# Eight of sixteen feature tiles of the retention output by seven products, and sums of stored tiles by GpSimd's queue

## The chip, the cores and the metric

One core of one Trainium2 chip runs the whole kernel in one launch. The metric is the time of one execution on the device in microseconds (us). The engines of the core are TensorE (PE, with its weight loads as PEld), VectorE (DVE), ScalarE (ACT), GpSimd (POOL) and SyncE (SP). Each runs its own instructions in order, and SP, ACT and POOL can issue DMA transfers from their own queues.

## The reference

Two layers over a sequence of 1024 tokens with 1024 features, batch 1, in float32: layer 0 mixes by forgetting attention, layer 1 by retention, and each is followed by a SwiGLU network with 2816 hidden features. The change lies mostly in retention:

```python
def retention(h, w_in, w_out):          # 4 heads, 512 value features each
    ...                                 # q, k, v, g from h @ w_in; q, k rotated
    _, y = lax.scan(step, state0, (qc, kc, vc))       # chunks of 64 tokens
    y = y.transpose(1, 0, 3, 2, 4).reshape(B, S, H, dv)
    mu = jnp.mean(y, axis=-1, keepdims=True)
    var = jnp.mean(jnp.square(y - mu), axis=-1, keepdims=True)
    y = ((y - mu) * lax.rsqrt(var + EPS)).reshape(B, S, H * dv).astype(h.dtype)
    return (jax.nn.silu(g) * y) @ w_out               # 2048 -> 1024 features

def swiglu(h, w_in, w_out):
    gu = h @ w_in
    return (jax.nn.silu(gu[..., :D_FF]) * gu[..., D_FF:]) @ w_out

def reference(x, ...):
    for i in range(DEPTH):
        h = rmsnorm(x, norm_mix[i])
        x = x + (forgetting_attention if i % 2 == 0 else retention)(h, ...)
        x = x + swiglu(rmsnorm(x, norm_ffn[i]), ffn_w_in[i], ffn_w_out[i])
    return rmsnorm(x, final_norm)
```

## The kernel before, in words

Activations lie with features on the 128 partitions and tokens along the free axis, in tiles of 128x512 (a half of the tokens, h = 0 or 1). Every float32 operand of TensorE is split in two parts, hi and lo: ACT casts the hi part (L98) and DVE subtracts it from the source to leave lo (L99). A product of two operands is then three matmuls, hi by hi, hi by lo and lo by hi. The plain form is `mm_u` (L101, matmuls at L106 to L108).

Most of the large projections don't use the plain form. They take a 2x2 block of (feature tiles x token halves) at a time and compute it by seven products instead of eight: `Blocks` loads four weight blocks A11 to A22 into two 128x1024 staging tiles (tag `st`, five buffers) and forms the sums S1 to S4 on DVE; the activations' side has B11, T1, T2, B21, T3, T4, B22, where the T's are sums of tiles of one feature pair; and `Products` (matmuls at L645 to L647) runs the seven pairs, each over four tiles of the inner dimension and three matmuls, into three PSUM banks. `Stored` keeps the seven activation operands of one group in DRAM; its `get` lands them in place by `landed`: a DMA on SP's queue writes the float32 tile into the buffer that will be lo, ACT casts hi out of it and DVE subtracts in place.

Each SwiGLU network stores its first 16 hidden tiles as two such groups (`stored[0]`, `stored[1]`, DRAM tiles named ac), and `paired_out` multiplies them with the output weights. Group 0 is landed while the last products of the input projection still run, group 1 while the last product of group 0 runs. The other six hidden tiles (ad) go through `mm_u`.

The retention layer runs eight stages (4 heads x 2 token halves). In `finish` of a stage ACT copies four value tiles out of PSUM, squares are summed, TensorE sums over the partitions (L159) and later spreads the per-token factors over all partitions (L165, tile rw in PSUM), DVE multiplies the four tiles by them (L1153) and they are stored to DRAM as zd. The gate silu(g) lies in DRAM as gd. For head 0 DVE multiplies it in at once (L1157); for the other 12 tiles it is loaded beside zd afterwards and DVE multiplies 128x1024 at a time (L801). The output projection is two passes over eight of the sixteen feature tiles each: the first (the loop at the end of the listing) is plain, eight output tiles x two halves x eight input tiles x three matmuls, and adds the residual xo; the second is `out_proj`, also plain.

The order of the instructions on each engine comes from a scheduler that moves them within dependences; the pools (`yp` with 16 buffers, `st` with 5, `bpa` with 32 and `bpb` with 24) limit how far ahead a load can be.

Of the kernel before, what the change touches and what calls it, by code (L numbers as in the profile page):

```python
# [17 lines left out]
P = 128  # L18
# [19 lines left out]
def trunk(ctx, tc, nc, d, out):  # L38
# [62 lines left out]
    def mm_u(ps, wts, acts, h, cols=slice(0, H), first=True, last=True):  # L101
        n = len(wts)
        for k in range(n):
            wh, wl = wts[k]
            xh, xl = (t[:, cols] for t in acts[k][h])
            nc.tensor.matmul(ps, wh, xh, start=(first and k == 0), stop=False)  # L106
            nc.tensor.matmul(ps, wh, xl, start=False, stop=False)  # L107
            nc.tensor.matmul(ps, wl, xh, start=False, stop=(last and k == n - 1))  # L108
# [76 lines left out]
    with ExitStack() as fs:  # L185
# [13 lines left out]
        wk0, wk1 = wtile(d["fox_qk"][1], 4), []  # L199
        for kt in range(KT):  # L200
# [7 lines left out]
            for at, w, idx, k in (0, wk0, 1, 4), (1, wk1, 3, 0), (3, wk1, 3, 4):  # L208
                if kt == at:
                    w += wtile(d["fox_qk"][idx][:, k * P:], 4)  # L210
# [285 lines left out]
    def landed(pool, src):  # L496

        hi, lo = units(pool)
        nc.sync.dma_start(lo.bitcast(F32), src)
# [9 lines left out]
    class Combos:  # L509
# [32 lines left out]
        def get(self, n):  # L542
# [4 lines left out]
    FROM_COMBOS = {"S2": ("B11", "T1", "T2"), "S3": ("B21", "T3"), "S4": ("T4", "B22")}  # L547
    FROM_STORED = {"A11": ("B11",), "S1": ("T1",), "S2": ("T2",), "A12": ("B21",), "S3": ("T3",), "A22": ("T4",),
                   "S4": ("B22",)}

    class Stored:


        def __init__(self, name, pools):
            self.pools = pools
            self.d = {n: dp.tile([P, 4 * H], F32, tag=name + n, name=name + n) for n in NAMES}
# [20 lines left out]

    class Blocks:


        def __init__(self, src):
            self.s1, self.ready = None, {}
            sts = []
            for i in range(2):
                st = sp.tile([P, 1024], F32, tag="st", name=nm("st"), bufs=5)
                nc.sync.dma_start(st, src[:, i * 1024:(i + 1) * 1024])
# [4 lines left out]
        def sums(self, early=False):  # L591
# [6 lines left out]
            nc.vector.tensor_tensor(self.s2, self.s1, self.a11, op=ALU.subtract)  # L598
# [6 lines left out]
        def get(self, n):  # L605
# [8 lines left out]
            if n == "S3":  # L614
                nc.vector.tensor_tensor(self.a21, self.a11, self.a21, op=ALU.subtract)
                return wsplit(self.a21)
            if n == "A12":
                return wsplit(self.a12)
# [51 lines left out]
    def in_turn(srcs, X, use, coming=None):  # L670
# [618 lines left out]
```

## Time and profile before

| | |
|---|---|
| time of the kernel, median of 3 runs | 2588.68 us (2587.34 to 2588.96) |
| time of the profiled execution | 2588.64 us |
| its span in the trace | 2586.9 us |
| TensorE busy | 2560.8 us, 99% of the span |
| DVE, ACT, POOL busy | 1839.0, 1228.3, 170.6 us |
| DMA traffic | 312.13 MB, mean 121 GB/s |

Busy time of TensorE counts overlapping matmuls: one 128x512 matmul lasts 0.39 us in the trace, but they start closer to each other than that, since they are pipelined. So the count of matmuls in a stretch tells its pace better than the busy share. The time of the profiled execution is 1.7 us above the span.

### The profile page before, as it was taken

How to read it: one execution, taken by the hardware profiler on the slowest of the kernel's cores; microseconds unless marked ns; L12 is line 12 of the kernel's file. 1: busy time of each engine (PE TensorE's matmuls, PEld its weight loads, DVE VectorE, ACT ScalarE, POOL GpSimd, SP SyncE). 2: the span in 40 equal slices, each digit the busy share in tenths (PEclk: the TensorE clock that was granted, in tenths of full speed). 3: DMA queues.
4: the chain of work that ended last, by engine and by line, in shares of the span. 5: the costliest groups of instructions: out<-in, count | busy, mean ns of one | idle time of the engine just before them, and what ended most of it. 6: DMA issues, size and time to landing. Idle time of an engine off the chain costs nothing.

```text
span 2586.9 us, 35264 instructions
## 1 busy us (share of the span) xinstructions
PE 2560.8 (99%) x12808; PEld 2182.2 (84%) x12808; DVE 1839.0 (71%) x3131; ACT 1228.3 (47%) x2320; POOL 170.6 (7%) x147
## 2 busy tenths in 40 slices
PE   9999999999999999999999999999999999999998
PEld 8889887888888878889898989898888888888888
DVE  6798888966666678886656576785567666668784
ACT  6566656543333454554343435662354333335543
POOL 0143323000000000001000010000000000000000
PEclk9999999999999999999999999999999999999999
DMA  3111142432332345533332325555522333325541
GB/s 130 45 58 58 58 147 93 152 106 94 114 106 94 122 155 176 166 116 115 102 118 98 110 98 167 184 191 193 202 98 82 110 98 107 103 90 186 175 143 66
DMA packets 145759, 312.13 MB, mean 121 GB/s; under 512 B 16560, under 2 KB 29616, under 8 KB 145584
## 3 DMA queue, kind: packets, MB, share of 16 engines
q1 hardware_dynamic: 144864, 309.33, 35.9%
q8 instruction: 100, 1.64, 0.3%
q14 instruction: 75, 0.61, 0.1%
q10 hardware_dynamic: 720, 0.55, 0.1%
HBM read 217.54 MB, written 92.27 MB: 120 GB/s over the span
## 4 chain that ended last, share of the span: by engine, by line
PE 93%; DVE 2%; DMA 2%; issue 2%; ACT 1%; POOL 0%; SPq 0%; DVEq 0%; POOLq 0%; ACTq 0%
PE mm L645 18%; PE mm L647 18%; PE mm L646 18%; PE mm L106 7%; PE mm L107 7%; PE mm L108 7%; PE mm L765 2%; PE mm L763 2%; PE mm L764 2%; PE mm L256 1%; PE mm L257 1%; PE mm L258 1%; DMA b<-ac_T 1%; PE mm L1116 1%; PE mm L1117 1%
## 5 line engine op out<-in xcount | busy, mean ns | idle before, releaser
L645 PE MATMUL mm<-b,wh 128*128 128x512 f32 x2128 | 826.7, 390 | 2.7 <-ACT b L98 2.7
L646 PE MATMUL mm<-b,wh 128*128 128x512 f32 x2128 | 827.9, 389 | 0.0
L647 PE MATMUL mm<-b,wl 128*128 128x512 f32 x2128 | 825.2, 389 | 0.0
L98 ACT CAST wh<-st 128x512 fp32r<-128x512 f32 (+1 forms) x449 | 276.6, 617 | 499.2 <-PE mm L646 298.3
L645 PEld LDWEIGHTS mm<-b,wh 128*128 128x128 f32 x2128 | 399.4, 188 | 86.5 <-ACT b L98 4.0
L647 PEld LDWEIGHTS mm<-b,wl 128*128 128x128 f32 x2128 | 399.5, 188 | 83.2 <-DVE wl L99 0.4
L646 PEld LDWEIGHTS mm<-b,wh 128*128 128x128 f32 x2128 | 399.6, 188 | 82.1
L99 DVE TENSOR_TENSOR wl<-st,wh 128x512 fp32r<-128x512 f32 (+1 forms) x449 | 318.6, 713 | 180.3 <-ACT wh L98 177.9
L98 ACT CAST wh<-s 128x512 fp32r<-128x512 f32 x252 | 156.5, 622 | 298.5 <-PE mm L646 270.6
L106 PE MATMUL mm<-b,wh 128*128 128x512 f32 x736 | 286.8, 393 | 7.8 <-ACT b L126 5.5
L107 PE MATMUL mm<-b,wh 128*128 128x512 f32 x736 | 287.4, 391 | 1.7 <-DVE b L99 1.7
L108 PE MATMUL mm<-b,wl 128*128 128x512 f32 x736 | 287.4, 391 | 0.0
L99 DVE TENSOR_TENSOR wl<-s,wh 128x512 fp32r<-128x512 f32 x252 | 180.2, 717 | 89.6 <-ACT wh L98 85.5
L106 PEld LDWEIGHTS mm<-b,wh 128*128 128x128 f32 x736 | 138.9, 189 | 37.3 <-ACT b L126 6.2
L107 PEld LDWEIGHTS mm<-b,wh 128*128 128x128 f32 x736 | 138.9, 189 | 29.5 <-DVE b L99 2.2
L108 PEld LDWEIGHTS mm<-b,wl 128*128 128x128 f32 x736 | 138.8, 189 | 28.4
L764 PE MATMUL mm<-wl,b 128*128 128x256 f32 x448 | 126.6, 283 | 0.0
L763 PE MATMUL mm<-wh,b 128*128 128x256 f32 x448 | 126.2, 283 | 0.0
L765 PE MATMUL mm<-wh,b 128*128 128x256 f32 x448 | 126.2, 283 | 0.0
L597 DVE TENSOR_TENSOR s<-st 128x512 f32<-128x512 f32 x84 | 58.2, 692 | 67.8 <-DMA st<-ffn_in 28.8
L98 ACT CAST b<-b 128x512 fp32r<-128x512 f32 x112 | 67.7, 620 | 71.9 <-DMA b<-ac_B 39.2
L99 DVE TENSOR_TENSOR b<-b,b 128x512 fp32r<-128x512 f32 x112 | 75.5, 688 | 33.0 <-ACT b L98 32.6
(500 smaller groups left out, 4019.7 us busy)
## 6 DMA issues: line engine op xcount, KB each, us to landing
st<-ffn_in SPq DMA_DIRECT2D x88, 512.0 KB, 3.5
st<-ffn_out_pairs SPq DMA_DIRECT2D x32, 512.0 KB, 3.6
b<-ac_T SPq DMA_DIRECT2D x64, 256.0 KB, 5.8
ac_T<-t SPq DMA_DIRECT2D x48, 256.0 KB, 2.4
b<-ac_B SPq DMA_DIRECT2D x48, 256.0 KB, 5.0
st<-fox_qk SPq DMA_DIRECT2D x32, 256.0 KB, 2.7
xo<-xd SPq DMA_DIRECT2D x32, 256.0 KB, 3.0
ac_B<-t SPq DMA_DIRECT2D x32, 256.0 KB, 2.4
```

What stands on the lines that cost most here:

```text
L98: nc.scalar.copy(hi, src)
L99: return nc.vector.tensor_tensor(lo, src, hi.bitcast(F32), op=ALU.subtract)
L106: nc.tensor.matmul(ps, wh, xh, start=(first and k == 0), stop=False)
L107: nc.tensor.matmul(ps, wh, xl, start=False, stop=False)
L108: nc.tensor.matmul(ps, wl, xh, start=False, stop=(last and k == n - 1))
L597: nc.vector.tensor_tensor(self.s1, self.a21, self.a22, op=ALU.add)
L645: nc.tensor.matmul(ps, hi[:, js], th, start=first and j == 0, stop=False, skip_group_check=True)
L646: nc.tensor.matmul(ps, hi[:, js], tl, start=False, stop=False, skip_group_check=True)
L647: nc.tensor.matmul(ps, lo[:, js], th, start=False, stop=(j == 3), skip_group_check=True)
L763: nc.tensor.matmul(o, th[:, tk], hi[:, js], start=f, stop=False, skip_group_check=True)
L764: nc.tensor.matmul(o, th[:, tk], lo[:, js], start=False, stop=False, skip_group_check=True)
L765: nc.tensor.matmul(o, tl[:, tk], hi[:, js], start=False, stop=(j == 3), skip_group_check=True)
```

## The change

Five parts.

1. The first pass of the retention output projection (now over heads 0 and 1) is done by seven products: `Blocks(w, True)` takes four weight tiles by strided loads, `Products` runs over them with a `Stored` group zc, and y is formed from the residual xo by adding or subtracting the products. Signs are chosen so that `finish` stores some tiles negated. The second pass (heads 2 and 3) stays plain.
2. The operands T1 to T4 of zc aren't computed on DVE: after each of heads 0 and 1, `zc.add` makes each by two transfers of GpSimd's queue, a copy from DRAM to DRAM and a transfer that adds to what lies there (16 transfers of 128x1024). SP loads the operands during and after the last three stages.
3. All 32 gate multiplies are moved into `finish` and onto GpSimd; the 8 at L1157 and the 12 at L801 on DVE go.
4. In each SwiGLU network, group 0 is loaded through staging tiles (128x1024 on SP) and then split; group 1 is still landed in place, but by GpSimd's queue (28 transfers of 128x512 in each network). So are eight tiles zd of the second pass, 128x512 each.
5. At the start the first weight load on SP is 128x128 instead of 128x512. At the end ACT copies the last tile's residual into PSUM before its matmuls, which then add to it; ACT squares straight from PSUM, and the column sum takes that square by matmuls of its own, two to a block of tokens where there was one.

```diff
-    def colsum(acc, mp, mtag, nb=4):
+    def colsum(acc, mp, mtag, nb=4, more=None):
...
-            nc.tensor.matmul(ps[:, b:b + 1], acc[:, b * P:(b + 1) * P], ones[:, 0:1], start=True, stop=True)
+            nc.tensor.matmul(ps[:, b:b + 1], acc[:, b * P:(b + 1) * P], ones[:, 0:1], start=True, stop=more is None)
+            if more is not None:
+                nc.tensor.matmul(ps[:, b:b + 1], more[:, b * P:(b + 1) * P], ones[:, 0:1], start=False, stop=True)
...
-        wk0, wk1 = wtile(d["fox_qk"][1], 4), []
+        wk0, wk1 = wtile(d["fox_qk"][1], 1), []
...
-    def landed(pool, src):
+    def landed(pool, src, queue):
...
-        nc.sync.dma_start(lo.bitcast(F32), src)
+        queue.dma_start(lo.bitcast(F32), src)
...
     class Stored:
...
+        def add(self, js, n, a, b):
+
+            c = slice(js.start * H, js.stop * H)
+            nc.gpsimd.dma_start(self.d[n][:, c], self.d[a][:, c])
+            nc.gpsimd.dma_start(self.d[n][:, c], self.d[b][:, c], accum_op=ALU.add)
+
         def get(self, n):
             if n not in self.t:
-                self.t[n] = [landed(self.pools[n], self.d[n][:, j * H:(j + 1) * H]) for j in range(4)]
+                if not self.staged:
+                    self.t[n] = [landed(self.pools[n], self.d[n][:, j * H:(j + 1) * H], self.queue) for j in range(4)]
+                    return self.t[n]
+                self.t[n] = []
+                for i in range(2):
+                    st = sp.tile([P, 1024], F32, tag="st", name=nm("st"), bufs=5)
+                    nc.sync.dma_start(st, self.d[n][:, i * 1024:(i + 1) * 1024])
+                    self.t[n] += [bsplit(self.pools[n], st[:, HALF[j]]) for j in range(2)]
             return self.t[n]
...
-        stored = [Stored(f"ac{i}_{g}_", pools) for g in range(2)]
+        stored = [Stored(f"ac{i}_{g}_", pools, g == 0) for g in range(2)]
...
+                if c1 == S and n == KT - 1:
+                    nc.scalar.copy(ps, u)
+                    mm_u(ps, ws[n], acts, h, cs, first=False, free=True)
+                    sq = sp.tile([P, H], F32, tag="sc", name=nm("sq"), bufs=4)[:, :wid]
+                    nc.scalar.activation(sq, ps, AF.Square)
+                    cps = colsum(norm.acc[h][:, cs], mp, "ms", nb, sq)
...
         for vt in range(4):
-            nc.vector.tensor_tensor(ys[vt], ys[vt], fb, op=ALU.mult)
-            if h < 1:
-                g = yu("g")
-                nc.sync.dma_start(g, gd[4 * h + vt][:, HALF[ib]])
-                nc.vector.tensor_tensor(ys[vt], ys[vt], g, op=ALU.mult)
-            nc.sync.dma_start(zd[4 * h + vt][:, HALF[ib]], ys[vt])
+            g = yu("g")
+            nc.sync.dma_start(g, gd[4 * h + vt][:, HALF[ib]])
+            if h < 2 and vt % 2 != ib:
+                nc.vector.scalar_tensor_tensor(ys[vt], ys[vt], -1.0, fb, op0=ALU.mult, op1=ALU.mult)
+            else:
+                nc.vector.tensor_tensor(ys[vt], ys[vt], fb, op=ALU.mult)
+            nc.gpsimd.tensor_tensor(ys[vt], ys[vt], g, op=ALU.mult)
...
+        if h < 2 and ib == 1:
+            js = slice(2 * h, 2 * h + 2)
+            zc.add(js, "T1", "B11", "B12")
+            zc.add(js, "T3", "B22", "B12")
+            zc.add(js, "T2", "T1", "B22")
+            zc.add(js, "T4", "T2", "B21")
...
-    for n in range(KT):
-        w = wtile2(d["ret_o"][n], 8)
-        for h in range(2):
-            ps = mm_ps()
-            mm_u(ps, w, acts, h)
...
+    prod = Products(blocks(0), zc).open()
+    for n in range(KT // 2):
...
+        prod.middle(lambda b: nc.scalar.copy(u["12"], b), closed)
+        nxt = Products(blocks(n + 1), zc, (acts, ACTS) if n == 2 else None).open() if n < 3 else None
+        prod.close()
...
+                nc.vector.tensor_tensor(t, xo, src, op=(ALU.add, ALU.subtract)[i])
```

How the change moves instructions shows at three places. On TensorE, in the first pass of the retention output projection, before (mm is the PSUM tile, b an activation part, wh and wl the weight's parts), these six rows stand where the second token half of the first output tile begins:

```order
L106 MATMUL mm_3445_17394<-b_3435_17374,wh_3443_17390 128x512
L107 MATMUL mm_3445_17394<-b_3436_17375,wh_3443_17390 128x512
L108 MATMUL mm_3445_17394<-b_3435_17374,wl_3444_17391 128x512
L106 MATMUL mm_3448_17423<-b_3398_17296,wh_3440_17384 128x512
L107 MATMUL mm_3448_17423<-b_3399_17297,wh_3440_17384 128x512
L108 MATMUL mm_3448_17423<-b_3398_17296,wl_3441_17385 128x512
```

At the like place of the change (L688 to L690 are the matmuls of `Products` there) the first product ends and the second begins:

```order
L688 MATMUL mm_3494_17538<-b_3378_17091,wh_3497_17541 128x512
L689 MATMUL mm_3494_17538<-b_3379_17092,wh_3497_17541 128x512
L690 MATMUL mm_3494_17538<-b_3378_17091,wl_3498_17542 128x512
L688 MATMUL mm_3495_17539<-b_3380_17096,wh_3505_17566 128x512
L689 MATMUL mm_3495_17539<-b_3381_17097,wh_3505_17566 128x512
L690 MATMUL mm_3495_17539<-b_3380_17096,wl_3506_17567 128x512
```

Before, an output tile of 128x512 took 24 matmuls into one bank; now a product takes 12, and seven products, 84 matmuls, make four output tiles.

On GpSimd, before, nothing stands between the rotation of the last keys and the program's end. In the change, these rows stand there from the second stage's end to the fourth's (zc.. are tiles in DRAM, L587 a copy, L588 an adding transfer, L1205 a gate multiply):

```order
L588 DMA zcT1_15290<-zcB12_15295 128x1024
L587 DMA zcT3_15291<-zcB22_15293 128x1024
L587 DMA zcT2_15289<-zcT1_15290 128x1024
L588 DMA zcT3_15291<-zcB12_15295 128x1024
L1205 TENSOR_TENSOR yt_3121_16141<-yt_3121_16141,g_3136_16184 128x512
L1205 TENSOR_TENSOR yt_3122_16144<-yt_3122_16144,g_3137_16189 128x512
L1205 TENSOR_TENSOR yt_3124_16149<-yt_3124_16149,g_3138_16194 128x512
L1205 TENSOR_TENSOR yt_3126_16154<-yt_3126_16154,g_3139_16199 128x512
L588 DMA zcT2_15289<-zcB22_15293 128x1024
L587 DMA zcT1_15290<-zcB11_15288 128x1024
L587 DMA zcT4_15294<-zcT2_15289 128x1024
L588 DMA zcT4_15294<-zcB21_15292 128x1024
```

The multiplies of a stage now stand behind the transfers of the head before, on the same queue and in order.

On GpSimd again, in the first SwiGLU network: these are the first of 28 rows that stood on SP before, behind the last of the attention's reductions.

```order
L376 ISA M_963_4734<-acc_942_4642 128x512
L501 DMA b_1847_9262<-ac0_1_B11_5495 128x512
L501 DMA b_1849_9267<-ac0_1_B11_5495 128x512
L501 DMA b_1851_9272<-ac0_1_B11_5495 128x512
L501 DMA b_1853_9277<-ac0_1_B11_5495 128x512
L501 DMA b_1867_9342<-ac0_1_T1_5497 128x512
L501 DMA b_1869_9347<-ac0_1_T1_5497 128x512
L501 DMA b_1887_9415<-ac0_1_B21_5499 128x512
```

The operands of group 1 are now issued by GpSimd, one 128x512 tile to a transfer, and SP's queue no longer holds them.

## Rows read from the trace of the kernel before

**Rows 1.** The page: busy time, share of the span and instructions of each engine.

```profile
PE 2560.8 (99%) x12808; PEld 2182.2 (84%) x12808; DVE 1839.0 (71%) x3131; ACT 1228.3 (47%) x2320; POOL 170.6 (7%) x147
```

**Rows 2.** Windows: stretch, its length, busy us (instructions) by engine, clock, DMA share, GB/s.

```profile
900.00:950.00 50.00, 48.19 (x210) 38.96 (x209) 39.42 (x64) 30.70 (x57) 0.00 (x0) 1.00 0.57 180
1000.00:1050.00 50.00, 49.07 (x217) 40.20 (x216) 43.75 (x73) 23.57 (x43) 0.00 (x0) 1.00 0.48 152
1800.00:1850.00 50.00, 50.00 (x222) 41.40 (x221) 31.80 (x43) 14.53 (x26) 0.00 (x0) 1.00 0.75 251
2400.00:2450.00 50.00, 50.00 (x222) 41.38 (x221) 39.42 (x64) 32.22 (x60) 0.00 (x0) 1.00 0.62 195
```

**Rows 3.** The chain of waits, 895 to 1015 us: start, us, what.

```profile
905.47 6.18 DMA b<-ac_T
...
930.77 5.33 DMA b<-ac_B
...
1008.01 5.09 DMA b<-ac_B
```

**Rows 4.** DMA issues: transfer, queue, count, KB each, median us to landing.

```profile
st<-ffn_in SPq DMA_DIRECT2D x88, 512.0 KB, 3.5
...
b<-ac_T SPq DMA_DIRECT2D x64, 256.0 KB, 5.8
...
zd<-yt SPq DMA_DIRECT2D x32, 256.0 KB, 3.0
st<-zd SPq DMA_DIRECT2D x16, 512.0 KB, 4.8
```

**Rows 5.** The chain of waits at the program's start.

```profile
1.16 3.52 DMA t<-xT
4.76 0.73 ACT b L126
5.54 1.43 PE mm L106 x2
```

**Rows 6.** The chain of waits after the last matmul of the last tile.

```profile
2575.58 0.43 DVE 22_4457_22642 L881
2576.04 0.42 ACT sq L138
2576.49 0.44 DVE acc L139
...
2577.06 0.59 PE cs L159 x4
```

**Rows 7.** Windows over the eight stages' ends (columns as in Rows 2).

```profile
1640.00:1780.00 140.00, 138.98 (x807) 124.47 (x805) 111.93 (x263) 82.41 (x180) 0.00 (x0) 1.00 0.57 190
```

**Rows 8.** Timeline of DVE from 1276 us: start, us, engine, line, operation.

```profile
1275.84 0.68 DVE L951 TENSOR_TENSOR m<-mm,cos 128x512 f32<-128x512 f32 x1
1276.44 1.45 DVE L99 TENSOR_TENSOR wl<-s,wh 128x512 fp32r<-128x512 f32 x1
1277.93 1.67 DVE L598 TENSOR_TENSOR s<-s,st 128x512 f32<-128x512 f32 x1
1279.52 0.68 DVE L684 TENSOR_TENSOR u<-mm,u 128x512 f32<-128x512 f32 x1
1280.12 0.68 DVE L99 TENSOR_TENSOR wl<-s,wh 128x512 fp32r<-128x512 f32 x1
```

**Rows 9.** Timeline of GpSimd in the same stretch.

```profile
1276.06 1.28 POOL L952 TENSOR_TENSOR m<-m,m 128x512 f32<-128x512 f32 x1 [69.79 <-DVE m L950]
1277.30 1.75 POOL L953 TENSOR_TENSOR m<-m,m 128x512 f32<-128x512 f32 x1
```

**Rows 10.** Timeline of TensorE where the factors of the fourth and fifth stage are spread.

```profile
1705.71 0.72 PE L165 MATMUL rw<-ident,yf 128*128 128x128 f32 x5
...
1719.08 0.72 PE L165 MATMUL rw<-ident,yf 128*128 128x128 f32 x5
```

**Rows 11.** Groups of instructions by line: busy us, mean ns.

```profile
L801 DVE TENSOR_TENSOR st<-st,st 128x1024 f32<-128x1024 f32 x12 | 14.7, 1224 | 8.4 <-DMA st<-gd 8.3
```

More of the change, by code (lines that the diff above doesn't have):

```diff
@@ L99, in split, with mm_u @@
         return nc.vector.tensor_tensor(lo, src, hi.bitcast(F32), op=ALU.subtract)
-    def mm_u(ps, wts, acts, h, cols=slice(0, H), first=True, last=True):
+    def mm_u(ps, wts, acts, h, cols=slice(0, H), first=True, last=True, free=False):
         n = len(wts)
@@ L105, in mm_u @@
             xh, xl = (t[:, cols] for t in acts[k][h])
-            nc.tensor.matmul(ps, wh, xh, start=(first and k == 0), stop=False)
-            nc.tensor.matmul(ps, wh, xl, start=False, stop=False)
-            nc.tensor.matmul(ps, wl, xh, start=False, stop=(last and k == n - 1))
+            nc.tensor.matmul(ps, wh, xh, start=(first and k == 0), stop=False, skip_group_check=free)
+            nc.tensor.matmul(ps, wh, xl, start=False, stop=False, skip_group_check=free)
+            nc.tensor.matmul(ps, wl, xh, start=False, stop=(last and k == n - 1), skip_group_check=free)
     HALF = (slice(0, H), slice(H, S))
@@ L543, in get, with __init__ @@
             return self.t[n]
-    FROM_COMBOS = {"S2": ("B11", "T1", "T2"), "S3": ("B21", "T3"), "S4": ("T4", "B22")}
     FROM_STORED = {"A11": ("B11",), "S1": ("T1",), "S2": ("T2",), "A12": ("B21",), "S3": ("T3",), "A22": ("T4",),
                    "S4": ("B22",)}
+    MAP4 = dict(zip(NAMES, (bpa, bpa, bpb, bpb, bpb, bpa, bpa)))
+    ACTS = {"A11": (6, 7), "S1": (0, 1), "A12": (2, 3), "S3": (4, 5)}
+    class Acts:
+        def __init__(self, srcs):
+            self.srcs, self.t = srcs, {}
+        def get(self, i):
+            if i not in self.t:
+                self.t[i] = load_units(bpb if i < 6 else bpa, self.srcs[i])
+            return self.t[i]
     class Stored:
-        def __init__(self, name, pools):
-            self.pools = pools
-            self.d = {n: dp.tile([P, 4 * H], F32, tag=name + n, name=name + n) for n in NAMES}
+        def __init__(self, name, pools, staged, names=()):
+            self.pools, self.staged = pools, staged
+            self.queue = nc.sync if names else nc.gpsimd
+            self.d = {n: dp.tile([P, 4 * H], F32, tag=name + n, name=name + n) for n in NAMES + names}
             self.t = {}
@@ L585, in __init__ @@
                 st = sp.tile([P, 1024], F32, tag="st", name=nm("st"), bufs=5)
-                nc.sync.dma_start(st, src[:, i * 1024:(i + 1) * 1024])
+                if neg:
+                    for t in range(2):
+                        nc.sync.dma_start(st[:, HALF[t]].rearrange("p (j c) -> p j c", j=4), src[i][:, t])
+                else:
+                    nc.sync.dma_start(st, src[:, i * 1024:(i + 1) * 1024])
                 sts.append(st)
@@ L791, in wtile2, with load_units @@
         return parts
-    def load_units(pool, src, gate=None):
-        r = []
+    def load_units(pool, src, inplace=True):
+        if inplace:
+            return [landed(pool, src[:, HALF[h]], nc.gpsimd) for h in range(2)]
         st = sp.tile([P, 1024], F32, tag="st", name=nm("st"), bufs=5)
         nc.sync.dma_start(st, src)
-        if gate is not None:
-            gt = sp.tile([P, 1024], F32, tag="st", name=nm("st"), bufs=5)
-            nc.sync.dma_start(gt, gate)
-            nc.vector.tensor_tensor(st, st, gt, op=ALU.mult)
-        for h in range(2):
-            r.append(bsplit(pool, st[:, HALF[h]]))
-        return r
+        return [bsplit(pool, st[:, HALF[h]]) for h in range(2)]
     def out_proj(wsrc, y, acts, xnew, gi, nextw, pools):
@@ L852, in gated @@
             nc.sync.dma_start(ad[f - 16][:, HALF[1]], c22)
-        in_turn([nw if f == 0 and nw else d["ffn_in"][i, f] for f in range(FT)], X, gated,
-                (stored[0], FROM_COMBOS))
+        in_turn([nw if f == 0 and nw else d["ffn_in"][i, f] for f in range(FT)], X, gated)
         y = paired_out(d["ffn_out_pairs"][i], stored, True, xold)
         wsrc = d["ffn_out"][i]
-        acts = [load_units(bpa if last else bpb, t) for t in ad]
+        acts = [load_units(bpa if last else bpb, t, False) for t in ad]
         if not last:
@@ L1075, in prepare @@
         kk, kt = load_k(h)
-        qq = [load_units(bpa, qd[h][e]) for e in range(2)]
+        qq = [load_units(bpa, qd[h][e], False) for e in range(2)]
         vv = [load_v(h, b) for b in range(TB)]
```

84 lines of the change are left out of this document (59 added, 25 removed).

## The prediction

> **What bounds the kernel now.** I read the page's busy line first: TensorE is busy for 99% of the span, DVE for 71%, ScalarE for 47%, GpSimd for 7% [rows 1]. So a change gains by taking matmuls away or by closing the few gaps between them, and loses by making TensorE wait. How much a matmul is worth is read in the windows: in 1800 to 1850 us, inside the pass that the change replaces, TensorE does 222 matmuls in 50 us without idling, and the same in the second SwiGLU network at 2400 to 2450 us [rows 2]. That is 0.225 us each, at a granted clock of 1.00.
>
> The windows also show where TensorE falls behind. In 900 to 950 us it does 210 and in 1000 to 1050 us 217, where 222 fit [rows 2]; both lie where the first network passes from input to output projection. The chain of waits runs there through landings of the stored operands, 6.18, 5.33 and 5.09 us long [rows 3]. The second network lost nothing at the like place.
>
> **The change part by part.** I make the sum against the profiled execution, 2588.64 us, which is 0.04 us from the median of the runs (2588.68) and holds a span of 2586.9 and 1.7 us outside it.
>
> *The products.* Before, 8 x 2 x 8 x 3 = 384 matmuls of 128x512; now 4 x 7 x 4 x 3 = 336. The 48 fewer are worth 48 x 0.225 = 10.8 us. By their duration of 0.39 us it would be 18.7 us, but they overlap, so the pace decides.
>
> *Group 0 of the networks.* Its landing in place starts only when the buffer is free, and the transfer then lies on the path. Staged, the transfer goes ahead and only the two splits are left. The loss at 900 to 950 us is 12 matmuls, 2.7 us, or 1.8 us by TensorE's idle time there (50 less 48.19) [rows 2]. I take 2.3 us off.
>
> *Group 1.* The 5 matmuls, 1.1 us, at 1000 to 1050 us stay: the operands are still landed in place, now by GpSimd's queue. The trace has no transfer from that queue. The nearest row is SP's landing of the same tile, 5.8 us [rows 4]. As three landings follow each other on the chain, one that is 0.5 us longer costs 1.5 us in the first network, while the second has room that the trace doesn't size. From below it costs nothing (the same transfers, and SP's queue is freer). From above, landings twice as long, 11.6 us, would put 5.8 us on each of the three, 17 us in each network. It is nearer to SP's row, as the same 16 DMA engines carry both: I add 1.5 us and keep 0 and 35 us as ends.
>
> The Trainium skill, page "DMA: Bandwidth & Descriptors", section "Anatomy of one DMA — SWDGE (gpsimd) path", fits a transfer of this queue by 2.0 us plus bytes over 436 GB/s. An estimate by it is 2.6 us for 256 KB, under SP's row; this term would be 0 and the sum below 2577.9 us. The trace holds no transfer of that queue to weigh it against.
>
> *The start.* The first matmul comes at 5.54 us, behind a transfer of xT of 3.52 us and ACT's cast [rows 5]. 192 KB less stand ahead of it; two transfers of 256 KB and one of 256 KB at the same time took 3.52 us, so 192 of 768 KB are at most 0.9 us. I take 0.5 us off, at least nothing.
>
> *The end.* From the last matmul DVE adds the residual (0.43 us), ACT squares (0.42), DVE adds the square (0.44), and the column sum takes 0.59 us [rows 6]. The two DVE steps go; two more short column sums come: 0.87 less 0.3, so 0.6 us off, at least 0.3.
>
> *The gates.* Off DVE go 8 multiplies of 0.6 us and 12 of 1.22 [rows 11]. GpSimd gets 32. It is beside DVE, but not free. At 1276 us GpSimd starts while DVE reads a PSUM tile (mm), and that one takes 0.68 us as ever; the next on DVE, with both inputs in SBUF, takes 1.45 instead of 0.68 us. GpSimd's own take 1.28 and 1.75 [rows 8, 9]. So a GpSimd multiply costs DVE up to some 1.1 us, and nothing where DVE works from PSUM, as the multiplications by the spread factor do. Four of these stand at each stage's end, which covers the first one or two of the four gates; I take 0.7 us each, ends 0.4 and 1.1.
>
> Now DVE over the eight stages, 1640 to 1780 us. It is busy 111.9 us with 263 instructions [rows 7]; each shows 0.08 us more than its pace (starts 0.60 apart at 0.68) [rows 8], so its need is 111.9 - 263 x 0.08 = 91 us of 140. By the order of the change, 27 more instructions of 128x512 (16 us) stand between the first and the last of these stages' factors, and four of 1.22 us fewer: 102. With 32 gates at 0.4, 0.7 and 1.1 it is 115, 125 and 137 us. So DVE stays under TensorE's time, but hardly so at the upper end, and stages wait for each other (squares, factor, gates, store). TensorE lost 1.0 us in these 140 before [rows 7]. I add 3 us, ends 0 and 12.
>
> The Trainium skill, page "SBUF — State Buffer", section "Who interferes with whom", says that a DVE instruction with two inputs in SBUF contends with a GpSimd one that reads SBUF, and that the second blocks fully. The trace agrees (1.45 us beside 0.68). By it all gates could stand at their dear end, 137 us, and the sum at 2588 us, the second rival below.
>
> *The sums by GpSimd's queue.* Copies from DRAM to DRAM and adding transfers aren't in the trace. The nearest rows are a store of 256 KB, 3.0 us, and a load of 512 KB, 4.8 us [rows 4]; one that reads and writes is at least 4.8 and, one after the other, 7.8 us. The queue waits inside: of the four transfers between the third and fourth stage's gates two follow from the one before, so 2 x 7.8 = 15.6 us stand in a gap between stages that is some 13 to 28 us (1705.71 to 1719.08 is a short one [rows 10]). That is hidden with little left: a tile that waits for its gate only holds its SBUF buffer. I take nothing, with 0 below. From above, at 12 us each the fourth stage's gates are some 8 us late, and the next ones again: up to 15 us.
>
> *The rest.* For each pair of output tiles the first pass needs four weight sums, seven splits and six sums from PSUM on DVE: 17 instructions, 11 us at 0.65, and splitting the second pass's inputs adds some 5 us; its seven products take 84 x 0.225 = 18.9 us. ACT's copies have room (14.5 of 50 us in 1800 to 1850 [rows 2]). That cover hides it: 0. Without it, with each of these on DVE 0.2 us longer, a pair would take DVE 20 us, and four pairs would cost 4 to 5 us.
>
> Sum: -10.8 - 2.3 + 1.5 - 0.5 - 0.6 + 3 = -9.7 us. I round the waits up by 0.5, for operands of zc that stand on SP ahead of stores: 2588.6 - 9.2 = **2579.4 us**.
>
> **The rivals.**
>
> *No new wait.* The gates and the queue are hidden: -10.8 - 2.3 - 0.5 - 0.6 = -14.2, and 2574.4 us. For it speaks that DVE has 49 us to spare in the stages; against it, that the contended instructions stand just where factors are awaited.
>
> *DVE becomes the bound in the stages.* Gates at 1.1 us and more, with waits in each stage: 12 us instead of 3, so 2588 us, no change. The need of 137 of 140 us speaks for it; it is against it that the network's stretch at 1000 to 1050 us runs DVE 43.75 of 50 us with 217 matmuls.
>
> *GpSimd's queue is the new wait: slower.* If landings of group 1 take 11.6 us by that queue, that is 35 us over both networks instead of 1.5, and 2579.4 + 33 = 2612 us; at half of the excess, 2595. It decides where the loss passes the gain of 9 us: six landings 1.5 us longer than I take, some 7.8 us each. For it: 28 transfers on one in-order queue in each network, from an engine whose plain multiply already takes 1.28 to 1.75 us [rows 9]. Against it: the buffers come free one by one, and the second network has room.
>
> *The products don't pay as they should* since an operand of zc lands late: T2 is needed about 8 us after the first product. One late adding transfer (12 us) ahead of the pass costs 5 to 10 us once, 2585 to 2589 us.
>
> **How the numbers follow.** My forecast, a net gain of some 5 to 12 us (2577 to 2584), gets 0.42; no new wait (2572 to 2577) 0.28; DVE as bound or a late zc 0.16 (2584 to 2592); GpSimd's queue 0.14 (2592 to 2612). The predicted time is that of the first. Both signs hold chances, but the larger ones leave 2 in 10 out if the range goes from 2571 to 2591: 0.02 below and most of the last case above. The likeliest one's own range is 2577 to 2584. A measurement of this kernel can tell about 0.2%, 5.2 us, from no change: faster is under 2583.5, slower above 2593.9. Faster takes the first two but a little (0.67) and some of the third (0.03): 0.7; slower 0.13; same 0.17.
>
> **What would show it.** In the changed profile: 48 matmuls of 128x512 fewer; 222 in 50 us within the new pass; 220 or more where 210 were, and 217 or a little less where 217 were; DVE instructions of 1.4 to 1.8 us beside GpSimd's gates, TensorE idle for 2 to 5 us over the eight stages; the first matmul at about 5.0 us. I am wrong if copies and adding transfers last over 10 us, if gates wait on them, if TensorE waits for landings from GpSimd's queue for more than 3 us in a network, or if DVE is busy without break through the stages.

## The result, and the profile after

The changed kernel takes 2600.6 us (2597.5 to 2603.2, 6 runs), the kernel before 2588.8 us (2587.3 to 2591.7, 6 runs): a ratio of 1.004, 95% interval 1.0029 to 1.005. It is slower by some 12 us and above my range, which ended at 2591 us; I had given "slower" 0.13. The profiled execution took 2603.23 us with a span of 2601.5, 14.6 us over that of before.

Where the time went shows in the windows of the changed kernel (stretch, length, busy us and instructions of PE, PEld, DVE, ACT, POOL, the clock, DMA share, GB/s). First the networks and the new pass, which answer to [rows 2]:

```profile
900.00:950.00 50.00, 50.00 (x222) 41.41 (x221) 40.37 (x66) 27.56 (x51) 0.00 (x0) 1.00 0.53 181
950.00:1000.00 50.00, 48.31 (x213) 39.71 (x212) 30.03 (x48) 26.27 (x47) 15.43 (x28) 1.00 0.59 198
1000.00:1050.00 50.00, 48.78 (x215) 40.03 (x215) 44.92 (x75) 24.73 (x44) 0.00 (x0) 1.00 0.34 113
1850.00:1900.00 50.00, 50.00 (x222) 41.40 (x221) 31.75 (x52) 21.39 (x37) 3.79 (x8) 1.00 0.53 179
2450.00:2500.00 50.00, 50.00 (x220) 40.86 (x219) 48.14 (x80) 22.79 (x42) 2.15 (x4) 1.00 0.41 138
```

The products run at full pace (222 in 1850 to 1900 us). The loss at 900 to 950 us is gone, but 9 and 7 matmuls are missing in the next two stretches: 16 where 17 were before. The second network has 2 fewer in its stretch, without idle time.

Then the stages, which answer to [rows 7]:

```profile
1660.00:1680.00 20.00, 17.16 (x88) 14.59 (x87) 16.06 (x34) 12.56 (x27) 7.33 (x6) 0.91 0.77 232
1680.00:1700.00 20.00, 20.00 (x119) 18.00 (x118) 18.66 (x32) 11.18 (x25) 7.74 (x8) 1.00 0.99 283
1700.00:1720.00 20.00, 15.52 (x88) 13.56 (x87) 13.80 (x32) 11.51 (x26) 7.29 (x6) 0.91 0.77 231
1720.00:1740.00 20.00, 20.00 (x117) 17.99 (x116) 16.38 (x34) 9.57 (x22) 8.65 (x9) 1.00 1.05 292
1740.00:1760.00 20.00, 15.31 (x95) 13.45 (x93) 12.55 (x24) 10.62 (x24) 6.08 (x6) 0.96 0.87 270
...
1640.00:1820.00 180.00, 161.85 (x870) 140.64 (x869) 148.37 (x293) 97.98 (x208) 51.78 (x46) 0.95 0.79 240
```

The same stretch before, whose last 40 us belong to the plain pass already:

```profile
1640.00:1820.00 180.00, 178.98 (x983) 157.57 (x982) 130.96 (x289) 90.02 (x194) 0.00 (x0) 1.00 0.59 194
```

TensorE idles 180 - 161.85 = 18.2 us there, and 1.0 us before. And the clock is 0.95 on average instead of 1.00, some 9 us more: it falls in slices with idle time or right behind one. Together about 26 us more. With the products' 10.8 us and the 0.6 and 0.8 us at start and end off, that is some 14 us, as between the two spans. (The DMA share counts the times of packets, so a slice can pass 1.)

A wait of those, read from its end, in the chain of waits of the changed kernel:

```profile
1694.93 10.24 DMA st<-vd
...
1705.20 0.74 ACT b L1071
...
1705.96 0.75 DVE b L1072
...
1706.74 3.08 DMA st<-vd
...
1710.47 0.58 ACT yt L1181
...
1711.09 0.80 PE mm L1172
```

A load of v takes 10.24 us, the next one 3.08. ACT casts it (L1071), and in order behind that it copies the value tiles out of PSUM (L1181); TensorE (L1172) waits for the bank. The timeline of TensorE there shows both prices, the idle time and the pace behind it:

```profile
1711.09 0.80 PE L1172 MATMUL mm<-b,b 128*128 128x512 f32 x1 [2.29 <-ACT yt L1181]
1711.68 0.63 PE L1173 MATMUL mm<-b,b 128*128 128x512 f32 x1
1712.11 0.63 PE L1174 MATMUL mm<-b,b 128*128 128x512 f32 x1
...
1716.85 0.39 PE L1172 MATMUL mm<-b,b 128*128 128x512 f32 x1
1717.07 0.39 PE L1173 MATMUL mm<-b,b 128*128 128x512 f32 x1
```

Behind the gap the matmuls start 0.43 us apart, the lower of the clock's two levels (1.2 GHz; the mean granted clock of 1700 to 1720 us is 0.91), and only later 0.22 to 0.23 again.

Such a wait isn't the sums' doing alone. In the lists of what TensorE waited for (us in total, times, longest), these two rows are the changed kernel's,

```profile
PE mm L1172 <- ACT yt L1181: 4.7, 2, 2.4
PE mm L1172 <- DVE wl L1151: 4.1, 1, 4.1
```

and this one is of the kernel without the sums (below):

```profile
PE mm L1172 <- ACT yt L1181: 4.4, 2, 2.3
```

There the loads of v just before these waits land in some 3 us, and the waits for ACT are as long. The plain pass with gates in the stages has them too (4.7 us, 2 times). What the kernel without the sums doesn't have is the second row, the longest single wait, 4.13 us at 1760.87 us. In the chain, two landings of operands of the products stand ahead of it:

```profile
1730.81 9.28 DMA b<-zcT
...
1746.17 6.19 DMA b<-zcT
```

The DMA rows of the page and of the changed kernel's list of issues (transfer, queue, KB each, median us to landing) answer to [rows 4]:

```profile
b<-ac_T POOLq DMA_DIRECT2D x32, 256.0 KB, 5.3
...
st<-vd SPq DMA_DIRECT2D x32, 256.0 KB, 4.5
g<-gd SPq DMA_DIRECT2D x32, 256.0 KB, 5.8
...
zcT<-zcB POOLq DMA_DIRECT2D x12, 512.0 KB, 8.1
...
zcB<-yt SPq DMA_DIRECT2D x16, 256.0 KB, 5.3
...
zcT<-zcT POOLq DMA_DIRECT2D x4, 512.0 KB, 6.8
```

And the load of v before:

```profile
st<-vd SPq DMA_DIRECT2D x32, 256.0 KB, 3.5
```

GpSimd's queue lands the same tile as fast as SP's did, and the sums' transfers take about what I had bounded them by (8.1 and 6.8 us against 4.8 to 7.8). But a load of v takes 4.5 us in the median instead of 3.5, and a stored value tile of heads 0 and 1 5.3 instead of 3.0: what runs beside the sums got slower.

And DVE and GpSimd at one stage's end, in their timelines (DVE first):

```profile
1686.24 0.68 DVE L1202 SCALAR_TENSOR_TENSOR yt<-yt,rw 128x512 f32<-128x512 f32 x1
1686.89 6.02 DVE L1187 TENSOR_TENSOR yacc<-yacc,sq 128x512 f32<-128x512 f32 x1
```

```profile
1687.05 5.31 POOL L1205 TENSOR_TENSOR yt<-yt,g 128x512 f32<-128x512 f32 x4
```

One sum on DVE with both inputs in SBUF took 6.02 us: it ended only after all four of GpSimd's multiplies, which follow each other without a gap. This sum (yacc, L1187) stands in the chain too, shortly ahead of the load of v that took 10.24 us.

### The profile page after: what moved, and what is told of

It reads as the page before. It is cut to its first block, busy times and chain, and to the rows that moved or that the text cites. A ratio compares the mean times of both kernels' runs of the same rounds, so it can differ in the third digit from the quotient of the medians.

```text
span 2601.5 us, 35380 instructions
## 1 busy us (share of the span) xinstructions
PE 2560.4 (98%) x12764; PEld 2179.3 (84%) x12764; DVE 1870.0 (72%) x3158; ACT 1250.7 (48%) x2358; POOL 266.0 (10%) x267
## 4 chain that ended last, share of the span: by engine, by line
PE 90%; DVE 3%; issue 3%; DMA 3%; ACT 1%; POOL 0%; SPq 0%; DVEq 0%; POOLq 0%; ACTq 0%
PE mm L689 19%; PE mm L690 19%; PE mm L688 19%; PE mm L106 6%; PE mm L107 6%; PE mm L108 6%; PE mm L808 2%; PE mm L806 2%; PE mm L807 2%; DMA st<-vd 1%; PE mm L260 1%; PE mm L259 1%; PE mm L258 1%; DMA b<-zcT 1%; DVE b L99 1%
## 5 line engine op out<-in xcount | busy, mean ns | idle before, releaser
L688 PE MATMUL mm<-b,wh 128*128 128x512 f32 x2240 | 870.2, 390 | 4.4 <-DVE 11_3499_17558 L1275 1.8
L690 PE MATMUL mm<-b,wl 128*128 128x512 f32 x2240 | 868.3, 390 | 0.0
L98 ACT CAST wh<-st 128x512 fp32r<-128x512 f32 (+4 forms) x446 | 274.4, 617 | 496.6 <-PE mm L689 344.1
L688 PEld LDWEIGHTS mm<-b,wh 128*128 128x128 f32 x2240 | 421.1, 188 | 92.7 <-ACT rs_a L144 2.2
L690 PEld LDWEIGHTS mm<-b,wl 128*128 128x128 f32 x2240 | 420.9, 188 | 87.6 <-DVE wl L99 0.7
L99 DVE TENSOR_TENSOR wl<-st,wh 128x512 fp32r<-128x512 f32 (+4 forms) x446 | 317.0, 714 | 180.8 <-ACT wh L98 178.0
L98 ACT CAST wh<-s 128x512 fp32r<-128x512 f32 x264 | 164.5, 624 | 334.4 <-PE mm L689 297.5
L99 DVE TENSOR_TENSOR wl<-s,wh 128x512 fp32r<-128x512 f32 x264 | 188.7, 716 | 100.5 <-ACT wh L98 96.4
L501 POOL DMA_DIRECT2D b<-ac_B x24 | 13.3, 553 | 1115.5 <-PE mm L689 1111.9
L98 ACT CAST b<-st 128x512 fp32r<-128x512 f32 (+1 forms) x128 | 73.9, 608 | 36.4 <-DMA st<-ac_T 11.5
```

What stands on the lines that cost most here:

```text
L98: nc.scalar.copy(hi, src)
L99: return nc.vector.tensor_tensor(lo, src, hi.bitcast(F32), op=ALU.subtract)
L688: nc.tensor.matmul(ps, hi[:, js], th, start=first and j == 0, stop=False, skip_group_check=True)
L690: nc.tensor.matmul(ps, lo[:, js], th, start=False, stop=(j == 3), skip_group_check=True)
```

## The experiments

Times are medians. The kernel before ran beside each group (2587.5 to 2589.3 us); between groups, differences of medians are uncertain by about 2 us, and the ratios to the kernel before stand with them. I began with two theories. A: the sums' transfers and the loads fill the DMA engines and hold the queues in the stages. B: GpSimd's gates hold up DVE.

**Gates back on DVE.**

```diff
-            nc.gpsimd.tensor_tensor(ys[vt], ys[vt], g, op=ALU.mult)
+            nc.vector.tensor_tensor(ys[vt], ys[vt], g, op=ALU.mult)
```

> The changed kernel with one line undone: the 32 gate multiplies of the stages run on DVE instead of GpSimd, all else as in the change (2600.6 us). Theory B (GpSimd's gates block DVE: 4 to 6 us of a stage's DVE time where the multiplies on DVE itself take 4 x 0.6 = 2.4) expects 2580 to 2588 us. Theory A (the sums by GpSimd's queue and the loads fill the DMA engines and hold SP and GpSimd in 1650 to 1800 us) expects 2596 to 2603 us, since the transfers are the same.

2609.0 us (ratio 1.0078, 1.0063 to 1.0093): slower by 8 still. The instructions' order changes with it, and why it is slower I can't say, but theory B as the main cause is out: with no multiply on GpSimd TensorE still idles 22 us in 1640 to 1820 us.

**No sums.**

```diff
-            zc.add(js, "T1", "B11", "B12")
-            zc.add(js, "T3", "B22", "B12")
-            zc.add(js, "T2", "T1", "B22")
-            zc.add(js, "T4", "T2", "B21")
+            for n, b in (("T1", "B12"), ("T3", "B12"), ("T2", "B22"), ("T4", "B21")):
+                zc.d[n] = zc.d[b]
```

> The changed kernel without the 16 transfers of GpSimd's queue that make T1 to T4; the operands T1 to T4 are loaded from B12, B22, B12 and B21 instead, as many loads of the same size, so the sums are left out of the result. Theory A expects the gap to close: 2578 to 2588 us, DMA share in 1660 to 1780 us down from 0.8 to 1.0 to about 0.6. Theory B expects 2597 to 2602 us.

2590.5 us (1.0004, 0.9995 to 1.0013). Without the sums it is 10 us faster, which speaks for theory A, but some 12 us of the loss are left. The scheduler's order changes here too: by the names of their tiles, some 4% of TensorE's and 10% of DVE's instructions in 1500 to 1950 us stand at another place. That holds in some measure for all experiments on the retention layer but the one with sums that nobody reads.

**Both.** The two edits together.

> Both of the edits before: gates on DVE and no sums (left out of the result). If the two costs add, 2574 to 2580 us, about what 48 matmuls fewer and the short ends are worth; if they are one and the same wait, the time of the better of the two alone.

2589.4 us (1.0006). Without the sums the gates' engine makes no difference. Something else loses 12 us.

**The retention layer of before** (plain first pass, gates as before, no sums; networks, start and end as in the change).

> The changed kernel with the retention layer of before (plain first pass, gates as before, no sums); the networks' operands, the start and the end are as in the change. If my terms for these hold: 2.3 - 1.5 + 0.5 + 0.6 = 1.9 us below before, 2586.9 us; by the windows of the changed profile (213 and 215 matmuls in the first network where 210 and 217 were, 2 fewer in the second) 0.2 - 0.4 + 0.5 + 0.6, some 2588 us. If GpSimd's queue in the networks is the loss, over 2593 us.

2585.7 us (0.999, 0.998 to 0.9999): 3.1 us under before. So the 15 us between this and the changed kernel are the retention layer's, which should have gained 10.8.

**Neither sums nor gates.** The edit that leaves the sums out, and:

```diff
-            g = yu("g")
-            nc.sync.dma_start(g, gd[4 * h + vt][:, HALF[ib]])
...
-            nc.gpsimd.tensor_tensor(ys[vt], ys[vt], g, op=ALU.mult)
```

> The changed kernel without the 16 transfers for the sums (T1 to T4 loaded from B12, B22, B12 and B21) and without the gates: the 32 gate tiles are neither loaded nor multiplied, both left out of the result. Theory C (what is left of the loss after the sums, some 15 us, comes from the gates: 24 more gate loads in the stages on SP's in-order queue, into the buffers that also hold the value tiles) expects 2573 to 2580 us. Theory D (it comes from the loads of the sums' operands and the strided weights in the last three stages) expects 2585 to 2591 us, as without the sums alone (2590.5).

2587.7 us (0.9993, 0.9983 to 1.0002): theory C falls, for this much at least. With only products and their loads the stages still lose 10 us and more.

**Gates alone**, on the plain pass.

> One part alone: all gates in the stages on GpSimd, as in the change, but the plain first pass of 384 matmuls and no stored group of the retention output. The like kernel with the gates of before took 2585.7 us. Theory C expects 2592 to 2600 us (the stages lose 8 to 15 us by the gates alone); theory D expects 2583 to 2588 us.

2594.3 us (1.0019, 1.001 to 1.0028), 8.6 us over the same kernel with the gates of before. On the plain pass the gates in the stages cost what theory C said.

**The sums on DVE**, from SBUF.

```diff
-            zc.add(js, "T1", "B11", "B12")
...
+                nc.sync.dma_start(e, zc.d["B11"][:, c])
+                nc.sync.dma_start(o, zc.d["B21"][:, c])
+                nc.vector.tensor_tensor(e, e, b12, op=ALU.add)
+                nc.vector.tensor_tensor(t, e, b22, op=ALU.add)
+                nc.vector.tensor_tensor(b12, b22, b12, op=ALU.add)
+                nc.vector.tensor_tensor(o, t, o, op=ALU.add)
```

> The changed kernel with the same sums made in another way: at the second stage of heads 0 and 1 SP loads B11 and B21 back, DVE makes T1 to T4 from them and the tiles in SBUF (16 sums of 128x512), SP stores them; no transfer from DRAM to DRAM and none that adds, and B12 isn't stored. If the sums cost what their removal gave (10 us) because of their traffic, this gives most of it back: 2588 to 2594 us. If any way of making them costs the same (SP waits for the operands anyway), 2598 to 2603 us.

2601.3 us (1.0047): no better. DMA share in 1640 to 1820 us falls from 0.79 to 0.72, DVE's busy time rises from 148 to 155 us. Less traffic and more work on DVE came to the same.

**The same, and gate tiles loaded by GpSimd's queue.**

```diff
-            nc.sync.dma_start(g, gd[4 * h + vt][:, HALF[ib]])
+            nc.gpsimd.dma_start(g, gd[4 * h + vt][:, HALF[ib]])
```

> The kernel with sums on DVE, and the 32 gate tiles loaded by GpSimd's queue, which has nothing else to do then, instead of SP's. Theory C's part that is SP's in-order queue (a gate load that waits for a buffer holds the loads of v behind it) expects 4 to 12 us less than with the loads on SP; if SP's order is not the point, within 3 us of it.

2608.3 us (1.0075): 7 us slower. So the place of the gate loads on SP's queue isn't shown to cost anything; on GpSimd's queue they stand in order with its multiplies. The stores that wait for a gate stayed on SP.

In the kernel with neither sums nor gates, in its timeline of DVE and that of TensorE below it, a stage's small steps stand behind the split of an operand of the products (b<-b) that had not landed:

```profile
1720.19 0.17 DVE L1193 TENSOR_SCALAR yv<-yv 128x4 f32<-128x4 f32 x1
1725.14 0.69 DVE L99 TENSOR_TENSOR b<-b,b 128x512 fp32r<-128x512 f32 x1 [4.78 <-ACT b L98]
1725.75 0.17 DVE L146 RECIPROCAL rs_b<-rs_a 128x4 f32<-128x4 f32 x1
```

```profile
1727.53 0.77 PE L167 MATMUL rw<-ident,yf 128*128 128x128 f32 x2 [3.25 <-DVE yf L1196]
```

That gave theory F.

**Operands through staging tiles, without sums and gates.**

```diff
-    zc = Stored("zc", MAP4, False, ("B12",))
+    zc = Stored("zc", MAP4, True, ("B12",))
```

> The kernel without sums' transfers and without gates (2587.7 us; both left out of the result), and one word changed: the 28 operands of the products are loaded through staging tiles, 512 KB each, and split from there, instead of being landed in place. Theory F (what is left of the loss is that ACT's and DVE's splits of an operand that lands in place stand, in order, ahead of the stage's own small steps, and wait for a landing of some 5 us) expects 2576 to 2583 us. Theory D' (it is the bytes and the DMA engines' time of these loads, wherever they land) expects 2585 to 2590 us.

2586.5 us (0.9995, 0.9986 to 1.0004): F falls as the main cause. TensorE still waits for the factor, and now for weights' splits too.

**The same edit on the changed kernel.**

> The changed kernel, sums and gates as in it, and only the operands of the products loaded through staging tiles instead of landed in place. Theory F expects 2590 to 2596 us (5 to 10 us below the changed kernel's 2600.6). If the waits then go to the staging tiles, which the loads of v and of the weights need too, 2598 to 2606 us.

2605.1 us (1.0064): slower, as the second expectation had it. In 1640 to 1820 us SP's queue waits 10.8 us for a staging tile that a weight's split still holds, and 12.6 us with an operand's load for a sum that isn't made yet.

**Gates of heads 2 and 3 with the second pass.**

```diff
-            nc.gpsimd.tensor_tensor(ys[vt], ys[vt], g, op=ALU.mult)
+            if h < 2:
+                nc.gpsimd.tensor_tensor(ys[vt], ys[vt], g, op=ALU.mult)
```

> The changed kernel with the gates of heads 2 and 3 as before: not in their stages but when the second pass loads its inputs (zd and gd to staging tiles, DVE multiplies 128x1024); heads 0 and 1 stay on GpSimd. The gates alone cost 8.6 us in the kernel with the plain pass (2594.3 against 2585.7); half of the gate loads go out of the last four stages. If the gates' loads and waits add to the loss there, 2592 to 2597 us; if the operands' landings hide it, 2599 to 2603 us.

2601.8 us (1.0051): nothing gained. The sums are made in stages 2 to 6, beside the gates of heads 0 and 1, which stay.

**That and the staging tiles.**

> Both: gates of heads 2 and 3 with the second pass, and the operands through staging tiles. If the two add, 2582 to 2590 us; if staging tiles are the short thing (v, weights, operands, zd and gd all take them), 2598 to 2606 us.

2602.1 us (1.005). No.

**A constant instead of the factor, without sums and gates** (theory G).

```diff
-        fb = rows(fac, mp, "ms")
+        fb = rows(rho[:, h, rs], mp, "ms")
```

> The kernel without sums' transfers and without gates (2587.7 us), and the value tiles multiplied by a constant column instead of the factor worked out from the column sums, so that nothing waits for the chain column sum, root, factor, spread (the factor is left out of the result too). In the kernel it is made from, TensorE waited 6.7 us in four places for that factor, and its clock was granted at half for some us behind such gaps. Theory G (the products' order of TensorE puts too little work between the column sum and the spreading of the factor) expects 2576 to 2582 us. If the waits only move to the next late tile, 2585 to 2590 us.

2579.9 us (0.9959, 0.9944 to 0.9974): 7.8 us faster. G holds for what is left when sums and gates are out, with the reserve that the order is another here too. The windows over 1640 to 1820 us, of the kernel with neither and then of this one:

```profile
1640.00:1820.00 180.00, 170.82 (x915) 149.62 (x914) 134.45 (x302) 101.35 (x213) 0.00 (x0) 0.97 0.53 163
```

```profile
1640.00:1820.00 180.00, 177.32 (x974) 155.93 (x973) 142.72 (x319) 106.64 (x226) 4.52 (x8) 1.00 0.57 178
```

Idle time falls from 9.2 to 2.7 us, and the clock comes back from 0.97 to 1.00, 5 us more.

**The same on the changed kernel.**

> The changed kernel, sums and gates as in it, with the same constant column instead of the factor (left out of the result). In the changed kernel's profile TensorE hardly waits for the factor but for value tiles' buffers and splits, so theory A (transfers of the sums and what queues behind them) expects little: 2594 to 2601 us. Theory G as the main cause of the whole loss expects below 2590 us.

2599.4 us (1.0033): 1.2 us. With sums and gates the factor is not what TensorE waits for.

**Sums that nobody reads.**

```diff
+            zc.add(js, "X1", "B11", "B12")
...
+            for n, b in (("T1", "B12"), ("T3", "B12"), ("T2", "B22"), ("T4", "B21")):
+                zc.d[n] = zc.d[b]
```

> The changed kernel with the 16 transfers of the sums made as before, but into tiles that nobody reads; T1 to T4 are loaded from B12, B22, B12 and B21 (the sums are left out of the result). If the sums' traffic on the DMA engines and on GpSimd's queue costs the 10 us, 2598 to 2602 us as the changed kernel; if it is the waiting for their results (SP's queue and the splits behind a late operand), 2589 to 2593 us as without the sums.

2604.4 us (1.0061, 1.0044 to 1.0078), no faster than with sums that are read. And the order of TensorE's, DVE's and ACT's instructions in the stages is the same as in the changed kernel, so this is the cleanest of the experiments. It isn't the wait for the sums' results; making them costs the time. Whether by their bytes, by what they hold on GpSimd's queue, or by the order that the scheduler chose with them in, it doesn't separate.

**Sums, but no gates.**

> The changed kernel, sums as in it, and only the gates left out (neither loaded nor multiplied; left out of the result). With sums and gates it takes 2600.6 us, without sums 2590.5, without both 2587.7. If gates and sums add, 2597.8 us; if the gates' multiplies and loads cost more beside the sums, because GpSimd's queue holds both and the loads share the DMA engines, 2590 to 2595 us.

2591.4 us (1.0011, 1.0001 to 1.002). The four cases, in us:

| | with sums | without sums |
|---|---|---|
| with gates in the stages | 2600.6 | 2590.5 |
| without gates | 2591.4 | 2587.7 |

Alone the sums cost 3.7 and the gates 2.8 us; together 12.9. So 6.4 us by the medians, 4.7 by the ratios, are due to their meeting. The DMA share in 1640 to 1820 us rises too, 0.53 with neither, 0.63 with gates, 0.73 with sums, 0.79 with both, and so does a load of v in the median, 3.2, 3.8, 3.7 and 4.5 us. But TensorE's idle time, 9, 9, 12 and 18 us, isn't in step with them, and with sums and no gates a load of v takes up to 9.38 us in a kernel that is 9 us faster than the changed one: the long load alone doesn't make the loss.

That the gates alone cost little is also because one wait takes another's place: with neither, TensorE waits 6.4 us for the factor, with gates 0.7 us for it and 4.4 for ACT's copies of the value tiles. On the plain pass, which hasn't the first of these waits, gates in the stages cost 8.6 us.

**The networks: group 1 through staging tiles**, on the retention layer of before.

```diff
-        stored = [Stored(f"ac{i}_{g}_", pools, g == 0) for g in range(2)]
+        stored = [Stored(f"ac{i}_{g}_", pools, True) for g in range(2)]
```

> The changed kernel with the retention layer of before (2585.7 us), and group 1 of the networks loaded through staging tiles on SP as group 0 is. In its profile the first network still does 211 and 220 matmuls in the two stretches of 50 us where 222 fit, while GpSimd's queue lands group 1: 13 matmuls, 2.9 us. If that is the in-place landing, 2582 to 2584 us, the fastest of all; if staging tiles run short there, 2586 to 2590 us.

2592.1 us (1.001): worse by 6 us. In 900 to 1050 us SP's queue waits 32.9 us with operands' loads for splits of weights, which hold the staging tiles; the first network does 203, the second 200 matmuls in a stretch of 50 us.

**Group 1 by SP's queue**, in place, on the retention layer of before.

```diff
-            self.queue = nc.sync if names else nc.gpsimd
+            self.queue = nc.sync
```

> The changed kernel with the retention layer of before (2585.7 us), and group 1 of the networks landed in place by SP's queue as before, instead of GpSimd's. If GpSimd's queue is what costs group 1 there (13 matmuls lost instead of the 5 of before), 2583 to 2585 us; if the queue makes no difference and only the buffers decide, 2585 to 2587 us.

2582.6 us (0.997, 0.9959 to 0.9982): the fastest kernel that computes everything, 3.1 us by the medians and 5 by the ratios (0.997 and 0.999) under the same with GpSimd's queue. Its landings aren't shorter (5.6 and 4.6 us in the median, 5.5 and 4.9 by GpSimd's queue). The chain of waits of the kernel with GpSimd's queue runs there from issue to issue:

```profile
978.87 0.51 POOL b L501
979.38 0.91 issue
980.30 0.54 POOL b L501
...
983.82 2.31 issue
986.15 3.22 DMA b<-ac_T
```

An issue takes GpSimd some 0.5 us, and between issues stand up to 2.31 us for which the profile shows no wait. That a transfer whose buffer isn't free holds those behind it is argued, not shown. With SP's queue, 950 to 1000 us is without a wait:

```profile
950.00:1000.00 50.00, 50.00 (x223) 41.39 (x222) 35.09 (x55) 28.43 (x52) 0.00 (x0) 1.00 0.60 184
```

## Why the prediction was wrong

Two steps failed, and they share the miss of 2600.6 - 2579.4 = 21.2 us about evenly.

One is the price of the sums and the gates. I took nothing for the sums' transfers and 3 us for the gates; together they cost 12.9 us, 9.9 more. For the sums I followed only what their transfers hold up on their own queue, and there the bounds were about right. I left out what else they move beside: the 16 DMA engines were at a share of 0.57 in the stages [rows 7], and gate loads, sums and operands were priced as if the loads beside them stayed as they were. And I held that a tile that waits for its gate only holds its SBUF buffer. Its store also stands on SP's in-order queue, which in 1640 to 1820 us waited 42.8 us for gates (41.3 us without the sums).

The other is a term that I didn't have: what the new order of TensorE's work does in the stages when it no longer covers the chain of the factor. With the 3 us for the gates off, the forecast is 2576.4 us, and the kernel with neither sums nor gates took 2587.7, 11.3 us more. Of these 7.8 go with the wait for the factor; the rest stays open.

Shown is that making the sums costs the time when nobody reads them as well as when they are read, that sums and gates together cost more than the two alone, and that loads of v are longer with them. What in the making of the sums costs it is not shown. The Trainium skill, page "DMA: Bandwidth & Descriptors", section "Issuing engines are not separate DMA queues", says that transfers of all issuing engines share the same 16 DMA engines; the longer landings agree with it. But the sums made on DVE lowered the DMA share to 0.72 and cost the same, which is against the engines' bandwidth alone. Two rivals stand: the places on SP's and GpSimd's in-order queues, and the scheduler's order, which differs in every kernel that leaves sums or gates out. No run kept the changed kernel's order and took the transfers out.

Point by point:

- *The products*, -10.8 us: the pace is as forecast, 222 matmuls in 50 us, and the count is 48 lower. The stages took the gain back.
- *The factor.* The prediction had no term for it. In the stages without sums and gates the wait for it is worth 7.8 us; that the new order leaves TensorE too little work between a column sum and the spreading is the reading that fits. In the changed kernel it hides behind the other waits (1.2 us).
- *The clock.* No term either. Behind a gap like that at 1711 us the matmuls come 0.43 us apart for a while, so 17 us more idle time cost 26 in all.
- *The gates.* DVE's need of 115 to 137 us was about right (by the same reckoning 148.37 - 293 x 0.08 = 125 us, though in 180 us), but four multiplies in a row hold a DVE instruction for all their length, 6.02 us beside 5.31, not for one at a time. The Trainium skill, page "SBUF — State Buffer", section "Who interferes with whom", calls the port pair that the two engines share an exclusive lock; the trace agrees, and here the DVE instruction waits for the whole row. But the second rival, DVE as the bound, isn't what happened: with the gates on DVE it is busy for less time, 139 instead of 148 of the 180 us, and the kernel is slower still. Why it is, by 8 us, stays open.
- *Groups 0 and 1.* -2.3 and +1.5 us: group 0 did what it should (222 where 210 were); group 1 gave it back, 7 to 9 matmuls in each of two stretches. GpSimd's queue costs 3 to 5 us in both networks together, above my 1.5, and not by longer landings, as the rival had it: they are as long as SP's, and the chain shows its issues, one behind the other.
- *Start and end*: the first matmul at 4.96 us instead of 5.54 (0.6; I took 0.5). At the end, from the last matmul to the scaling of the column sums:

```profile
2591.87 0.39 ACT sq L922
2592.31 0.38 PE cs L161 x2
...
2593.18 0.17 DVE rv L934
```

1.31 us where [rows 6] took 2.1 up to the end of the column sum: 0.8 less, and I took 0.6.

The rival whose time came nearest was the third, GpSimd's queue as the new wait, 2595 to 2612 us. It holds the result by luck: it spoke of longer landings in the networks, and the loss is in the retention layer. The fourth, an operand of zc that lands late, came in part: the 4.13 us at 1760.87 us, in the stages and not in the pass.

## What to carry to other kernels

Price a moved transfer by what runs beside it, not only by its own queue: where engines wait in order for loads, further traffic can lengthen the very loads that the bound engine waits for (here 3.5 to 4.5 us in the median). Two additions that each fit into a stage's spare time need not fit together, so measure them apart and together. An edit that leaves something out can change the scheduler's order too; an edit that keeps the work and only drops its use, as the sums that nobody reads, is the cleaner test. And a gap of the bound engine costs more than its length where its clock falls behind it.

## What the runs showed of the hardware

GpSimd instructions of two SBUF inputs that follow each other without a gap held off a DVE instruction of the same kind for all of them (6.02 us beside four of 1.3 us each). Copies within DRAM and transfers that add there took 8.1 us in the median for 512 KB from GpSimd's queue, with a DMA share of 0.77 to 1.05 around them. After idle gaps of 2.37 us (1665.81 us) and 2.29 us (1711.09 us) TensorE's matmuls came 0.43 us apart for some 3 us, at the lower of its two levels, and at 0.22 to 0.23 after that. It isn't so after every gap: in the kernel with sums and no gates, after one of 2.24 us (1711.27 us), they came 0.23 us apart at once.
